# A fifth pair of weight blocks by seven products in the first output product, and new places for the sums made in memory

## The chip, the core and the metric

The kernel runs on one core of a Trainium2 chip. The metric is the device time of one execution, in microseconds; of several executions of one kernel the median is given. All data are 32-bit floats.

## The reference

One layer of an encoder for 256 tokens of 2048 features, cut to the steps that matter:

```python
h = rms_norm(x, attn_norm)
qa, ka, va, qb, kb, vb, ga, gb = split(h @ w_in)
ya = windowed_gqa(qa, ka, va)            # 8 heads of 128
yb = dilated_attention(qb, kb, vb)       # 3 groups of 4 heads, merged to 4 x 128
merged = sigmoid(ga) * (ya @ w_branch_a) + sigmoid(gb) * (yb @ w_branch_b)
x = x + merged @ w_out                   # the output product: 2048 x 2048
hf = rms_norm(x, ffn_norm)
g = dwconv(hf @ w_ffn_gate)
x = x + (gelu(g) * (hf @ w_ffn_up)) @ w_ffn_down
x = x + sigmoid(rms_norm(x, ple_norm) @ w_ple_gate) * (p @ w_ple_proj)
return rms_norm(x, final_norm)
```

The weights dominate: the stream of all their blocks is 258 pieces of 1 MB. The change touches `merged @ w_out`.

## The kernel before

**Precision.** A float32 operand is split in two parts, `hi` (rounded to the matmul's own type) and `lo` (the rest), and a product is made of three matmuls: hi x hi, hi x lo, lo x hi. ScalarE makes `hi` of the weights (L287), VectorE makes `lo` (L288).

**Jobs and pieces.** All matrix products stand in one list of jobs (`_plan`), and their 128x128 weight blocks in one stream (`_stream`), cut in these pieces of 16 blocks. A piece is loaded as two halves of 8 blocks on SP's queue (`load`, L264), into six buffers `raw`; a half is then split into `whi` and `wlo`, of four buffers each (`split_to`). TensorE takes what has been split and releases the buffers. So the whole stream runs as far ahead of TensorE as the buffers let it.

**What is done between.** Everything that is no matmul of the stream is attached to a step of a job: `at((i, k), f)` runs `f` in the program when job `i` comes to its step `k` (`run_due`). The order of the instructions on each engine follows this program order, but a scheduler may move an instruction ahead of or behind others where operands and buffers allow it; instructions in `keep(...)` stay in program order. The jobs that the change speaks of are 34 to 36 (queries), 37, 41, 45 and 47 (`ba`, the branch-A product in four quarters, 8 steps each), 39, 42, 46 and 48 (`bb`, branch B, 4 steps each), 38, 40, 43 and 44 (`gab`, the gates, 16 steps each), and 49 and 50 (`o`, the output product in two halves of its columns, 16 steps each).

**Seven products.** The jobs with eight column blocks (`o`, `gab`, `v8`, `d0`, `d1`, `pgs`) go through `seven_product`. It takes a pair of row blocks of the weights at a time (a piece: 2 row blocks x 8 column blocks) against a pair of feature blocks and the two halves of the tokens. Taken plainly, a pair is eight block products of 128x128 by 128x512, so 24 matmuls. For the pairs in `seven` it uses a scheme with seven block products, so 21 matmuls, in four parts; it needs sums of the weight blocks and sums of the activations. `_pairs` gives the order of the pairs and which go by seven. The partial results are spread over the outputs by `spread_sums`, once, after the last pair by seven of the job (`done`).

- *Sums of weights.* For the jobs before the feed-forward part they are made in memory: `sums_in_memory(j)`, for the j-th pair by seven of the stream, at the step that `MADE_AT[j]` names. It puts a small marker on ScalarE (L330) and POOL (L331), so that the transfers are not issued too soon, and then issues transfers on POOL's queue: a copy of 512 KB (L336), for `w_out` a copy of 256 KB more (L339), two additions in memory of 256 KB (L340, L341) that wait for the copies, and for `w_out` a third (L343) that waits for these. `back` fetches the 512 KB on SP's queue into a buffer `sums` (L356), of which there are three; for `w_out` the other 256 KB go into the second half of the pair's `raw` (L273). The first three fetches of the output product are at step 0 of job 49 (L1152 and L1153), each later one behind part 1 of a pair by seven. The buffers `sums` lie in the pool `ff`, which takes the memory of the attention pool that is closed there (L1146).
- *The four parts.* Part 0 is 4 blocks of `raw`, part 1 the 8 blocks of `sums`, part 2 the first 8 blocks of `raw`, part 3 four blocks that VectorE adds up (L298). TensorE uses them in this order.
- *Sums of activations.* For the output product `add_up` makes them and `early` holds them, as `hi` and `lo`. `merge` calls it: it turns the gated sum `m` by transposes on TensorE (L1022) and splits it into `merged`; from pair 4 (`LATER`) on it also adds up. The merges of quarter 2 are at step 4 of job 47, those of quarter 3 at step 2 of job 49.

Of the kernel before, what the change touches and what calls it, by code (L numbers as in the profile page):

```python
# [10 lines left out]
F32 = mybir.dt.float32  # L11
FR = mybir.dt.float32r
AF = mybir.ActivationFunctionType
ALU = mybir.AluOpType
AX = mybir.AxisListType

P = 128
T = 256
# [19 lines left out]
SUB = 8  # L38
QUARTERS = KC // 4
# [20 lines left out]
def _plan():  # L60
# [48 lines left out]
    for half in range(2):  # L109
# [7 lines left out]
        for c in range(2):  # L117
# [5 lines left out]


TOGETHER = 3
AHEAD = 8 + 5 + 4 * 4
SAVED = 8
SPLIT = 4
ROWS = 7
SHL = 6  # L130
LATER = 4
# [3 lines left out]
FETCHED = ((24, 8), (28, 8), (32, 8), (36, 8), (38, 9), (38, 14), (49, 8), (49, 12))  # L135
MADE_AT = [(9, 1), (10, 8), (11, 14), (13, 4), (14, 12), (16, 14), (18, 2),
           (19, 4), (19, 9), (19, 14), (20, 8), (21, 3), (23, 8), (25, 8), (27, 12), (30, 0), (31, 14),
           (34, 0), (37, 0), (38, 4), (38, 11), (39, 2), (40, 6), (40, 12), (41, 3), (43, 4), (43, 11), (44, 5), (46, 0)]


def _pairs(kind, c):

    if kind == "pgs":
        return [0, 1, 4, 5, 2, 6, 7, 3], range(4, 8)
    if kind == "v8":
        return [0, 1, 2, 4, 3, 5, 6, 7], FARS
    if kind == "gab":
        return [0, 4, 1, 2, 6, 3, 5, 7], GATED
    if kind == "o":
        return ([2, 4, 5, 6, 7, 0, 1, 3] if c else [0, 1, 2, 4, 5, 6, 7, 3]), range(LATER, LATER + 4)  # L150
    if kind == "d1" and c == 1:
        return [5, 0, 1, 6, 2, 3, 7, 4, 8, 9, 10], range(5)
    return [8, 0, 1, 2, 3, 9, 4, 5, 6, 7, 10], range(SAVED)
# [62 lines left out]
def _encoder(ctx: ExitStack, tc, xt, pt, cols, table, onehot, mask, ident_in, last_gain, wts, xrows, out):  # L216
    nc = tc.nc
# [3 lines left out]
    big = ctx.enter_context(tc.tile_pool(name="big", bufs=2))  # L221
# [33 lines left out]
    held = {}  # L255
# [89 lines left out]
    def early_row():  # L345
        return ap_.tile([P, W4], F32, name="row", tag="qf", bufs=4)
# [239 lines left out]
    def at(i, f, *a):  # L586

        due.setdefault(i, []).append((f, a))
# [97 lines left out]
    def view(a, offset, *dims):  # L686
        return bass.AP(tensor=a.tensor, offset=a.offset + offset, ap=[a.ap[0], *([step, n] for step, n in dims)])
# [188 lines left out]
    def add_up(two, out, spare=None):  # L876

        s = (spare_row() if spare is None else spare).rearrange("p (b n) -> p b n", n=P)
        nc.vector.tensor_tensor(view(s, 0, (W4 // 2, 2), (1, P)), view(two, 3 * P, (-3 * P, 2), (1, P)),
                                view(two, P, (0, 2), (1, P)), op=ALU.subtract)  # L880
        nc.vector.scalar_tensor_tensor(s[:, 1], s[:, 0], -1.0, two[:, 0, :P], op0=ALU.mult, op1=ALU.subtract)
        nc.vector.tensor_tensor(s[:, 3], two[:, 1, :P], s[:, 1], op=ALU.add)
        hi, lo = out
        nc.scalar.activation(hi, s, AF.Copy)
        nc.vector.tensor_tensor(lo, s, hi.bitcast(F32), op=ALU.subtract)
# [32 lines left out]
    def spare_row():  # L918
        return row() if "ff" in held else early_row()
# [2 lines left out]
        return [held["shl"][m >= SHL][:, c, :, m % SHL, :] for c in range(2)]  # L922

    def early(m):
        return [held["early"][:, c, :, m - LATER, :] for c in range(2)]

    def row():
        return held["ff"].tile([P, W4], F32, name="row", bufs=ROWS)
# [7 lines left out]
    def spread_sums(kind, n, bank, end, when):  # L936

        by = [rooted(kind, t) for t in range(2)]

        def put(t, c, a):  # L940
            if end and c:
                q = quarter(n, t, c)
                nc.vector.scalar_tensor_tensor(q, a, by[t], q, op0=ALU.mult, op1=ALU.add)
                return
            if kind != "o":
                nc.scalar.activation(a, a, AF.Copy, scale=by[t])
            to_residual(n, t, c, a)

        first, u, v, w = [row() for _ in range(4)]
        nc.scalar.activation(first, bank["p1"], AF.Copy)  # L950
        nc.vector.tensor_tensor(u, bank["p6"], first, op=ALU.add)
        nc.vector.tensor_tensor(v, bank["p7"], u, op=ALU.add)
        for a, b in ((u, u), (w, v)):
            nc.vector.scalar_tensor_tensor(a, bank["p5"], -1.0, b, op0=ALU.mult, op1=ALU.subtract)
        todo = [(0, 0, first), (1, 0, v), (0, 1, u), (1, 1, w)]
        if kind == "o":
            for a in todo:
                put(*a)
            return
        for a, e in zip(todo, when):  # L960
            at(e, put, *a)
# [73 lines left out]

    def rooted(kind, t):
        return 1.0 if kind == "o" else rc[1][:, t:t + 1]

    def joined(n, t, acc, by):

        r = res[:, t, n * W4:(n + 1) * W4]
        nc.vector.scalar_tensor_tensor(r, acc, by, r, op0=ALU.mult, op1=ALU.add)
# [95 lines left out]
    for i, job in enumerate(_JOBS):  # L1138
# [42 lines left out]
        if kind == "gg":  # L1181
            held["asked"] = AHEAD
        if kind == "gg" or (kind == "g" and n == FHALF):
# [2 lines left out]
                j = i + late + (9 * e // 4 if late else 5 * e // 2)  # L1186
                sums_ahead((j, 4), (j + 2, 4))
        if kind == "ba" and n == QUARTERS - 1:
            held["early"] = big.tile([P, 2, 4, QUARTERS, P], FR, name="early", tag="mov", bufs=1)
        if kind == "u" and n % FHALF == FHALF - 2:  # L1190
            for e in range(3):
                at((i, 8), back)
# [52 lines left out]
        elif kind in ("o", "d0", "d1", "gab", "pgs", "v8"):  # L1245
# [3 lines left out]
            if (kind, n) == ("gab", 0):  # L1249
                tags.update(p3="sp", p4="sp", c22="acc", p1="acc", p6="pt", p7="pt", p5="misc")  # L1250
            still, sums_at = {"o": (stills["o"], early), "gab": (stills["v"], of_input), "pgs": (stills["pg"], of_residual),
                               "v8": (stills["v"], of_first)}.get(
                kind, (lambda k: held["act"][:, k, :], shl))
# [23 lines left out]
        elif kind in stills:  # L1277
            tag = {"pg": ("acc", "pt"), "pp": ("sp", "acc"), "ba": ("acc", "sp" if n == 1 else "acc"), "bb": ("pt" if n == 0 else "sp", "pt" if n == 1 else "acc")}[kind][n % 2]
# [18 lines left out]
        elif kind in ("gab", "pgs", "v8"):  # L1297
            th = held["th", "pp" if kind == "pgs" else n]
            for name, a, t in (("p2", "ga", 0), ("p3", "gb", 0), ("p4", "ga", 1), ("c22", "gb", 1)):
# [9 lines left out]
                if n == 0 and a == "ga":  # L1309
                    m = held["m"][:, t, :]  # L1310
# [3 lines left out]
        elif kind in ("o", "d0", "d1"):  # L1314
            parts = held["ss1" if kind == "o" else "ss2"]
            for name, t, c in (("p2", 0, 0), ("p3", 0, 1), ("p4", 1, 0), ("c22", 1, 1)):
                if end:
                    joined(2 * n + c, t, acc[name], rooted(kind, t))
                    squares_of(2 * n + c, t, parts)
                elif kind != "o" and name == "c22":  # L1320
                    joined(2 * n + c, t, acc[name], rooted(kind, t))
                else:
                    a = row()
                    nc.scalar.activation(a, acc[name], AF.Copy, scale=rooted(kind, t))
                    to_residual(n, t, c, a)
            if kind != "d0" and not end:
                at((i + 1, 10), first_squares, parts)
        elif kind == "pg":
            if last:
                last_gates(n, acc, rest)  # L1330
            else:
                for t in range(2):
                    gate(n, t, acc[t], last)
            if n == QUARTERS - 2:
                so_far()
        else:
            after(job, i, acc)
# [51 lines left out]
```

## Time and profile before

| | |
|---|---|
| median of 3 runs | 1443.12 us (1443.11 to 1444.47) |
| the profiled execution, its own time | 1444.3 us |
| its span, first to last instruction | 1442.5 us |
| granted TensorE clock, mean | 0.998 of full speed |
| busy: TensorE, VectorE, ScalarE, POOL | 1431.2, 1183.9, 876.3, 188.3 us |
| moved by DMA | 397.31 MB, 275 GB/s over the span |

The profile is of one execution. Times are in microseconds from the start of the span. A line of the order of time gives the start, the duration, the engine, the source line, the instruction, output and inputs, the number of such instructions, and in brackets the engine's idle time before it with what ended it. "SPq" and "POOLq" are the sequencers that issue transfers. Matmuls are pipelined: the start of one to the start of the next is what one costs, not its duration. A line of the windows gives the stretch, its length, the busy time of TensorE, its weight loads, VectorE, ScalarE and POOL, the granted clock, the busy share of the DMA engines and the GB/s.

### The profile page before, as it was taken

The numbers are of one execution on the slowest core, as the hardware profiler recorded it, in microseconds if no ns is written. First come the engines' busy times: TensorE is split into PE (matmuls) and PEld (weight loads), VectorE is DVE, ScalarE is ACT, GpSimd is POOL, SyncE is SP. The second block draws the span as 40 slices with busy tenths as digits, with TensorE's granted clock in tenths as the row PEclk, the third lists the DMA queues.
The fourth block names the chain that finished last, engine by engine and source line by source line (L and its number), as shares of the span: only waits on it lengthen the run. The fifth ranks groups of instructions, "written<-read, shape, count | busy, mean of one in ns | idle before, by whom it ended". The sixth has DMA issues, their size and how long they took to land.

```text
span 1442.5 us, 21000 instructions
## 1 busy us (share of the span) xinstructions
PE 1431.2 (99%) x7452; PEld 1227.1 (85%) x7452; DVE 1183.9 (82%) x1635; ACT 876.3 (61%) x1256; POOL 188.3 (13%) x291
## 2 busy tenths in 40 slices
PE   9999999999999999999999999999999999999997
PEld 8898888888888888888888888888888888888886
DVE  7798966668879878878888878997888887998896
ACT  7576654456656656775555556776555555677864
POOL 0022222111222110201111100102111110010000
PEclk9999999999999999999999999999999999999999
DMA  9798998889999978968888887989988888799672
GB/s 327 252 244 255 301 292 247 253 231 295 293 295 320 279 238 301 300 220 301 301 287 296 288 300 243 266 292 299 310 307 303 314 302 295 250 294 285 211 240 93
DMA packets 128149, 397.31 MB, mean 275 GB/s; under 512 B 14628, under 2 KB 19876, under 8 KB 127916
## 3 DMA queue, kind: packets, MB, share of 16 engines
q1 hardware_dynamic: 93372, 300.79, 60.4%
q0 software_dynamic: 32656, 91.24, 24.4%
q10 hardware_dynamic: 2016, 3.94, 0.9%
q8 instruction: 58, 0.95, 0.3%
q14 instruction: 47, 0.39, 0.1%
HBM read 363.11 MB, written 58.76 MB: 292 GB/s over the span
## 4 chain that ended last, share of the span: by engine, by line
PE 95%; DVE 2%; DMA 1%; ACT 1%; issue 0%; SPq 0%; POOLq 0%; DVEq 0%; ACTq 0%
PE acc L395 29%; PE acc L398 15%; PE acc L475 12%; PE acc L476 12%; PE acc L474 12%; PE acc L423 3%; PE acc L425 3%; PE acc L424 3%; PE first L372 2%; DMA raw<-in_wts 1%; DVE wlo L288 1%; PE pt L987 1%; PE pt L754 1%; PE acc L447 0%; ACT whi L287 0%
## 5 line engine op out<-in xcount | busy, mean ns | idle before, releaser
L288 DVE TENSOR_TENSOR wlo<-raw,whi 128x1024 fp32r<-128x1024 f32 (+2 forms) x581 | 660.8, 1158 | 94.9 <-ACT whi L287 87.2
L287 ACT ACTIVATE whi<-raw 128x1024 fp32r<-128x1024 f32 (+2 forms) x581 | 573.5, 1005 | 234.6 <-PE acc L476 92.0
L395 PE MATMUL acc<-mov,whi 128*128 128x512 f32 x1840 | 441.3, 391 | 0.0
L395 PEld LDWEIGHTS acc<-mov,whi 128*128 128x128 f32 x1840 | 337.8, 188 | 65.5
L398 PEld LDWEIGHTS acc<-mov,wlo 128*128 128x128 f32 x1840 | 237.3, 191 | 9.0 <-ACT mov L531 0.2
L398 PE MATMUL acc<-mov,wlo 128*128 128x256 f32 x1840 | 243.1, 283 | 0.0
L512 ACT ACTIVATE t<-acc 128x256 f32<-128x256 f32 x115 | 43.6, 379 | 149.6 <-PE acc L395 149.6
L476 PE MATMUL acc<-whi,mov 128*128 128x512 f32 x259 | 100.8, 389 | 0.0
L475 PE MATMUL acc<-wlo,mov 128*128 128x512 f32 x259 | 100.8, 389 | 0.0
L474 PE MATMUL acc<-whi,mov 128*128 128x512 f32 x259 | 100.6, 390 | 0.0
L288 DVE TENSOR_TENSOR wlo<-sums,whi 128x1024 fp32r<-128x1024 f32 x62 | 75.5, 1219 | 8.9 <-ACT whi L287 8.9
L474 PE MATMUL acc<-whi,act 128*128 128x512 f32 x207 | 80.9, 391 | 0.0
L475 PE MATMUL acc<-wlo,act 128*128 128x512 f32 x207 | 80.7, 390 | 0.0
L476 PE MATMUL acc<-whi,act 128*128 128x512 f32 x207 | 80.7, 390 | 0.0
L287 ACT ACTIVATE whi<-sums 128x1024 fp32r<-128x1024 f32 x62 | 65.4, 1056 | 20.4 <-PE acc L476 9.4
L934 POOL DMA_DIRECT2D x<-row x33 | 28.5, 908 | 310.8 <-PE acc L476 106.0
L325 POOL DMA_DIRECT2D kept<-sums x33 | 17.8, 540 | 360.2 <-DVE sums L321 219.4
L475 PE MATMUL acc<-wlo,merged 128*128 128x512 f32 x164 | 64.1, 391 | 0.3 <-DVE wlo L288 0.2
L474 PE MATMUL acc<-whi,merged 128*128 128x512 f32 x164 | 64.0, 390 | 0.0
L476 PE MATMUL acc<-whi,merged 128*128 128x512 f32 x164 | 63.9, 389 | 0.0
L857 ACT ACTIVATE c<-c 128x256 f32<-128x256 f32 x44 | 18.3, 417 | 67.2 <-DVE c L855 67.2
L476 PEld LDWEIGHTS acc<-whi,mov 128*128 128x128 f32 x259 | 48.6, 188 | 10.1
(274 smaller groups left out, 2147.9 us busy)
## 6 DMA issues: line engine op xcount, KB each, us to landing
raw<-in_wts SPq DMA_DIRECT2D x452, 512.0 KB, 6.0
sums<-kept SPq DMA_DIRECT2D x62, 512.0 KB, 5.8
kept<-in_wts POOLq DMA_DIRECT2D x66, 256.0 KB, 8.0
sums<-in_wts POOLq DMA_DIRECT2D x33, 512.0 KB, 7.3
kept<-sums POOLq DMA_DIRECT2D x33, 512.0 KB, 4.6
raw<-in_wts SPq DMA_DIRECT2D x64, 256.0 KB, 5.2
kept<-in_wts POOLq DMA_DIRECT2D x29, 512.0 KB, 7.7
x<-row POOLq DMA_DIRECT2D x33, 256.0 KB, 7.9
```

The lines of the kernel that those rows point to most:

```text
L287: nc.scalar.activation(hi, src, AF.Copy)
L288: ins = nc.vector.tensor_tensor(lo, src, hi.bitcast(F32), op=ALU.subtract)
L372: nc.tensor.matmul(firsts[e][:, T * low:], w, m[:, :2 * T - T * low], start=(k == 0 and not low), stop=(k == KC - 1 and low != turned), sk ...
L395: nc.tensor.matmul(acc, hi[:, k, :], m, start=(first and k == 0), stop=(last and k == SUB - 1), skip_group_check=True)
L398: nc.tensor.matmul(acc[:, T:], lo[:, k, :], m[:, :T], start=False, stop=False, skip_group_check=True)
L423: nc.tensor.matmul(acc, xh, hi, start=(k == 0), stop=False)
L424: nc.tensor.matmul(acc, xh, lo, start=False, stop=False)
L425: nc.tensor.matmul(acc, xl, hi, start=False, stop=(k == n - 1 - t * late))
L474: nc.tensor.matmul(acc, xh, hi, start=(e == 1), stop=False)
L475: nc.tensor.matmul(acc, xh, lo, start=False, stop=False)
L476: nc.tensor.matmul(acc, xl, hi, start=False, stop=(e == uses[name]))
L512: keep(nc.scalar.activation(t, acc[:, T:], AF.Copy, scale=scale))
```

## The change

In half 0 of the output product pair 3 joins the pairs that go by seven products, and pair 2 takes its place as the last pair, by eight. The order becomes 0, 1 by eight, 3, 4, 5, 6, 7 by seven, 2 by eight (before: 0, 1, 2 by eight, 4, 5, 6, 7 by seven, 3 by eight). Half 1 is left as it is. Pair 3 of `merged` was split long before, so its sums of activations are made by a new function, `again`, from `hi` + `lo` of pair 3; it is called at step 4 of job 47. The buffer `early` has one place more.

There is one more set of sums in memory, 30 for 29 (`AHEAD`). The first 17 places in `MADE_AT` stay; the last twelve become thirteen. For the same j: (36, 4) for (37, 0), (37, 4) for (38, 4), (38, 2) for (38, 11), (38, 9) for (39, 2), (39, 2) for (40, 6), (40, 6) for (40, 12), (41, 3) as before, (42, 2) for (43, 4), (43, 6) for (43, 11), (44, 4) for (44, 5), (45, 6) for (46, 0), and (47, 2) new. Since pair 3 comes in between, the sets from (38, 9) on belong to a pair by seven that stands one earlier in the order than the set of the same number before.

```diff
-AHEAD = 8 + 5 + 4 * 4
+AHEAD = 9 + 5 + 4 * 4
...
-           (34, 0), (37, 0), (38, 4), (38, 11), (39, 2), (40, 6), (40, 12), (41, 3), (43, 4), (43, 11), (44, 5), (46, 0)]
+           (34, 0), (36, 4), (37, 4), (38, 2), (38, 9), (39, 2), (40, 6), (41, 3), (42, 2), (43, 6), (44, 4), (45, 6), (47, 2)]
...
-        return ([2, 4, 5, 6, 7, 0, 1, 3] if c else [0, 1, 2, 4, 5, 6, 7, 3]), range(LATER, LATER + 4)
+        return ([2, 4, 5, 6, 7, 0, 1, 3], range(LATER, SUB)) if c else ([0, 1, 3, 4, 5, 6, 7, 2], range(LATER - 1, SUB))
...
-        return [held["early"][:, c, :, m - LATER, :] for c in range(2)]
+        return [held["early"][:, c, :, m - LATER + 1, :] for c in range(2)]
...
+    def again(m):
+        two = spare_row().rearrange("p (c t) -> p c t", t=T)
+        hi, lo = (held["merged"][0][:, 2 * m:2 * m + 2, c:c + T].bitcast(F32) for c in (0, T)) if 2 * m < SPLIT else (
+            held["merged"][1][:, 2 * m - SPLIT:2 * m - SPLIT + 2, c:c + T].bitcast(F32) for c in (0, T))
+        nc.vector.tensor_tensor(two, hi, lo, op=ALU.add)
+        add_up(two, early(m))
...
-            held["early"] = big.tile([P, 2, 4, QUARTERS, P], FR, name="early", tag="mov", bufs=1)
+            held["early"] = big.tile([P, 2, 4, QUARTERS + 1, P], FR, name="early", tag="mov", bufs=1)
+            at((i, 4), again, LATER - 1)
```

## The prediction

> **What bounds the kernel now.** I read the page first, then the idle time of TensorE, then the order of time around the output product.
>
> ```profile
> span 1442.5 us, 21000 instructions
> PE 1431.2 (99%) x7452; PEld 1227.1 (85%) x7452; DVE 1183.9 (82%) x1635; ACT 876.3 (61%) x1256; POOL 188.3 (13%) x291
> ...
> PE 95%; DVE 2%; DMA 1%; ACT 1%; issue 0%; SPq 0%; POOLq 0%; DVEq 0%; ACTq 0%
> ```
>
> TensorE is busy for 99% of the span and carries 95% of the chain of waits. So a matmul less is time won at its full pitch, and any late operand in front of TensorE is time lost. There is almost nothing else to win. Now the order of time on TensorE at the first output product (the job "o", half 0), whose pairs stand in the order 0, 1, 2 by eight and then 4, 5, 6, 7 by seven.
>
> ```profile
> 524.05 1.03 PE L1022 MATMUL pt<-ident,m 128*128 128x128 f32 x8
> ...
> 535.84 0.39 PE L474 MATMUL acc<-whi,merged 128*128 128x512 f32 x1
> ...
> 541.28 1.03 PE L1022 MATMUL pt<-ident,m 128*128 128x128 f32 x8
> ...
> 547.63 0.39 PE L474 MATMUL acc<-whi,merged 128*128 128x512 f32 x1
> ...
> 548.31 0.39 PE L474 MATMUL acc<-whi,merged 128*128 128x512 f32 x1
> 548.54 0.39 PE L475 MATMUL acc<-wlo,merged 128*128 128x512 f32 x1
> ...
> 553.07 0.39 PE L474 MATMUL acc<-whi,merged 128*128 128x512 f32 x1
> ...
> 553.75 0.39 PE L474 MATMUL acc<-whi,early 128*128 128x512 f32 x1
> ```
>
> The 0.39 us is the latency of one matmul; they overlap. A pair by eight is 24 matmuls: from 535.84 to 541.28 that is 5.44 us, 0.2267 us each, and from 547.63 to 553.07 again 5.44. So three pairs take three equal steps, apart from the eight transposes at 541.28. The first pair by seven starts at 553.07 and its first matmul that needs the sums fetched from memory (the second of its four parts, against `early`) starts at 553.75. TensorE waits for nothing here.
>
> **The change part by part.** *Matmuls removed.* Pair 3 goes by seven products: 21 matmuls for 24, so 3 x 0.2267 = **-0.68 us**. It lies wholly on the bound engine. That is 0.05% of the time; a measurement of this kernel can tell about 0.2% (2.9 us) from no change.
>
> *The new sums of activations* (`again`, at step 4 of the last branch-A job, after two merges at the same step). It issues on VectorE one 128x512 add, the three small operations of `add_up` and one 128x512 subtraction, and on ScalarE one 128x512 copy. The merges of before show the same operations:
>
> ```profile
> 527.10 0.42 DVE L879 TENSOR_TENSOR row<-row 128x256 f32<-128x256 f32 x1
> 527.55 0.29 DVE L881 SCALAR_TENSOR_TENSOR row<-row 128x128 f32<-128x128 f32 x1
> ...
> 528.09 0.29 DVE L882 TENSOR_TENSOR row<-row 128x128 f32<-128x128 f32 x1
> ...
> 529.49 1.29 DVE L885 TENSOR_TENSOR early<-row,early 128x512 fp32r<-128x512 f32 x2
> 530.70 1.28 DVE L1011 SCALAR_TENSOR_TENSOR m<-th,acc 128x512 f32<-128x512 f32 x2
> 531.90 2.35 DVE L288 TENSOR_TENSOR wlo<-raw,whi 128x1024 fp32r<-128x1024 f32 x2
> ```
>
> 0.65 for the add (half of the pair of 128x512 operations at 529.49), 0.42 + 0.29 + 0.29, and 0.65: 2.3 us. Queued behind it on VectorE are the two low halves at 531.90. With 2.3 us more the first of them ends at 531.90 + 1.17 + 2.3 = 535.4. They belong to the first two half-pieces of the output product (four buffers of `wlo`, three half-pieces of 2.7 us ahead of TensorE at that time), so TensorE needs the first at 535.84 + 0.23 = 536.07. I take nothing; the cover is about 0.7 us, and if VectorE runs 1 us later than this it costs 0.3. The range of this term is 0 to 0.5.
>
> *The first pair by seven comes one pair sooner.* This is the term that decides. The sums of weights of the first three pairs by seven are fetched by three transfers at the start of this job (`back`, on SP's queue). They go into buffers whose memory belonged to the attention part, and come free only when the last merge's transposes have read it:
>
> ```profile
> 541.36 0.33 SPq L264 DMA_DIRECT2D raw<-in_wts  x1
> 542.35 1.60 SPq L356 DMA_DIRECT2D sums<-kept  x3
> 549.29 0.33 SPq L264 DMA_DIRECT2D raw<-in_wts  x1
> ```
>
> The issue at 542.35 follows the end of the transposes (541.28 + 1.03 = 542.31) at once. These transposes stand at the same step in the changed kernel, so the issue stays where it is. What took the data in:
>
> ```profile
> 549.28 1.06 ACT L287 ACTIVATE whi<-sums 128x1024 fp32r<-128x1024 f32 x1 [1.92 <-DMA sums<-kept]
> ```
>
> ```profile
> 550.37 1.23 DVE L288 TENSOR_TENSOR wlo<-sums,whi 128x1024 fp32r<-128x1024 f32 x1 [0.56 <-ACT whi L287]
> 551.51 0.68 DVE L298 TENSOR_TENSOR raw<-raw 128x512 f32<-128x512 f32 x1
> ```
>
> ScalarE already waits 1.92 us for that first transfer, until 549.28; the low half is done at 551.60, and TensorE needs it at 553.75 + 0.23 = 553.98. Before, 2.4 us of slack hide this. In the changed kernel pair 3 by seven starts at 547.63, and its low half of the sums is needed at **548.54**, 5.44 us sooner. The slack of 2.4 becomes a lack of 3.1 us if the transfer lands as before.
>
> It should land somewhat sooner. The raw load issued at 541.36 (first half of the third pair by seven) stood ahead of the sums. In the changed kernel its buffer comes free only after pair 3's third part, which itself waits for the sums, so it goes behind them. What 512 KB are worth there shows in the transfers between 528 and 560 us, in 40 slices of 0.8 us:
>
> ```profile
> GB/s 205 207 356 251 31 20 0 31 225 277 197 317 238 36 0 179 282 184 179 97 259 341 410 425 415 425 415 282 154 197 282 149 269 292 261 294 187 161 294 213
> ```
>
> From 545.6 to 549.6 it runs at about 415 GB/s, so 512 KB take 1.26 us. The first sums then land at about 549.2 - 1.25 = 547.95. The ends: as before (549.2) where the order does not help, and 546.9 where the load ahead cost twice that. From landing to a finished low half it takes 551.60 - 549.28 + 0.1 = 2.4 us, so the wait is 547.95 + 2.4 - 548.54 = 1.8 us (0.8 to 3.1).
>
> Behind it VectorE is next late: the 128x512 add (0.59 until the next can start) and the low half of the third part (1.17) come after it, 1.75 us, while TensorE has six matmuls, 1.36 us. That adds 0.4. After this VectorE can keep up, but with little to spare:
>
> ```profile
> 535.80:553.10 17.30, 17.30 (x82) 14.37 (x82) 14.26 (x22) 9.22 (x12) 0.00 (x0) 1.00 0.71 250
> 553.10:572.10 19.00, 19.00 (x85) 15.74 (x84) 17.37 (x19) 15.17 (x17) 0.18 (x1) 1.00 0.89 305
> ```
>
> The second row is the four pairs by seven: VectorE (third value) is busy 17.37 of 19.00 us. The fifth such pair in a row costs nothing more by itself; the larger traffic (share of the DMA engines 0.89) fits too. So this step costs 1.8 + 0.4 = **+2.2 us** (1.2 to 3.5).
>
> *The sets of sums in memory.* One more set of five transfers on POOL's queue, and twelve at other steps, all at the same step or sooner for the same number. How long a set takes:
>
> ```profile
> 509.20 1.14 POOL L331 TENSOR_TENSOR edges<-edges,mhalf 128x1 f32<-128x1 f32 x1 [18.15 <-ACT edges L330]
> 510.29 0.56 POOL L336 DMA_DIRECT2D kept<-in_wts  x1
> ...
> 517.00 0.86 POOL L340 DMA_DIRECT2D kept<-in_wts  x1 [5.61 <-DMA kept<-in_wts]
> ...
> 525.09 0.80 POOL L343 DMA_DIRECT2D kept<-kept  x1 [6.36 <-DMA raw<-in_wts]
> ```
>
> The last set of before starts at 509.20 and issues its last addition at 525.09; the additions of that line land in 6.5 us (the line's own times to landing, shortest, median and longest),
>
> ```profile
> DMA to landing us min/median/max: 5.2/6.5/7.8
> ```
>
> so it is done at 532. In the changed kernel this is the last but one, two steps earlier (about 506.5), and the new last one follows on POOL from about 522.4, issues its last addition at 538.3 and is done at 545. Its sums are fetched for the fourth pair by seven of half 1, past 580. So nobody waits for it, and it costs nothing as a wait. Nothing is queued behind it on POOL before the first rows added to the residual, past 570. Behind the ScalarE marker of each set stands only the next split.
>
> As traffic, the moves go into stretches with room (eighth value, the share of the DMA engines):
>
> ```profile
> 300.00:320.00 20.00, 20.00 (x107) 17.13 (x106) 12.53 (x18) 11.39 (x18) 2.40 (x4) 1.00 0.72 198
> 320.00:340.00 20.00, 20.00 (x91) 16.57 (x90) 16.10 (x18) 11.08 (x14) 3.32 (x4) 1.00 0.80 219
> 340.00:360.00 20.00, 19.69 (x86) 15.67 (x85) 17.37 (x22) 12.56 (x15) 2.77 (x4) 1.00 1.02 358
> ...
> 520.00:540.00 20.00, 20.00 (x94) 16.64 (x93) 16.57 (x25) 10.77 (x13) 0.80 (x1) 1.00 0.69 196
> ```
>
> One place can go either way. After the set that starts at 325 us a raw load lands late and TensorE loses about 0.6 us:
>
> ```profile
> 333.45 9.81 DMA raw<-in_wts
> ```
>
> ```profile
> 345.89 0.39 PE L474 MATMUL acc<-whi,merged 128*128 128x512 f32 x1
> 346.51 0.50 PE L475 MATMUL acc<-wlo,merged 128*128 128x512 f32 x1 [0.24 <-DVE wlo L288]
> ```
>
> 345.89 to 346.51 is 0.62 for 0.23. The sets there move up by 7 to 25 us, and one of five transfers takes the place of one of four. I take nothing, with -0.6 to +1.0 as ends.
>
> [...]
>
> **The sum.** -0.68 + 2.2 + 0 + 0 = **+1.5 us**. Against the profiled execution (1444.3 us, 1442.5 of it span) that gives 1445.8; that execution lies 1.2 above the median of the runs, 1443.12, so for the median I say **1444.6**.
>
> **Rivals.** *No wait.* The sums land by 546.1, because the loads ahead were the whole delay (3.8 us from the issue would do). The eight fetches of sums between 530 and 600 us took:
>
> ```profile
> DMA to landing us min/median/max: 4.5/6.7/8.4
> ```
>
> Then only -0.68 is left, or -1.3 if the loss at 345.89 goes too: 1442.4 to 1441.8. For it: the shortest is near 3.8. Against it: none is under it, and the two loads issued just before 541 stay ahead. Chance 0.24.
>
> *Slower, by the late sums.* If the first sums land after 549.3 the wait of 3.2 and the 0.4 behind it outweigh the gain by 2.9. The place is the same; the cause would be the last additions of the new set (538 to 545) on the engines that bring the two raw pairs and the sums, or a later issue on SP. At 550.3: 4.2 + 0.4 - 0.7 = +3.9, so 1447.0. For it: the 9.81 us load beside a set. Against it: the share of 0.69 between 520 and 540. Chance 0.20.
>
> *Faster by more than the matmuls.* The losses beside the moved sets all vanish and none comes in their place: it would take 2.2 us beyond -0.68, and the rows above show TensorE idle for 0.3 us of the 20 from 340 and for none in the others. Chance 0.04: 1440.
>
> **How the numbers follow.** My forecast (+0.3 to +2.8, so 1443.4 to 1445.9) has 0.52, no wait 0.24, slower 0.20, faster 0.04. Within 0.2% are the first two, 0.76. The range reaches from the no-wait case less a little (1441.8) to the middle of the slower one (1446.8).
>
> **What would show it.** Right: at the output product three matmuls less, TensorE and ScalarE both waiting at pair 3's sums, a gap of 1 to 3 us after about 548.3, then one of 0.4, and none in the later pairs by seven. Wrong: no gap there (then I misread what holds the transfer back), a gap at 536 (then `again` is not covered), or raw loads that land late between 310 and 360 or 520 and 545.

## The result and the profile after

The changed kernel takes **1451.1 us** (median of four runs, 1450.41 to 1451.68) beside 1443.3 us for the kernel before on the same chip: a ratio of 1.0048, with a 95% interval of 1.0036 to 1.006. It is 7.8 us slower where +1.5 was forecast. Its profiled execution took 1450.99 us, 1448.9 of it span, so 6.4 us more span than before. (The rest of the 7.8 is 0.3 us more outside the span, 2.1 for 1.8, and that the profiled execution of before lies 1.0 us above its median and this one 0.1 below.) The places below are found in that execution.

The page of the changed kernel: the span and the busy times.

```profile
span 1448.9 us, 21022 instructions
...
PE 1433.7 (99%) x7449; PEld 1227.1 (85%) x7449; DVE 1188.3 (82%) x1643; ACT 878.7 (61%) x1260; POOL 190.5 (13%) x297
```

There are three matmuls fewer (7449 for 7452), and yet TensorE is busy for 2.5 us longer: matmuls that take longer are among the loss, not only waiting. Here is the order of time on TensorE in the changed kernel, from the end of part 0 of pair 3, the first pair by seven.

```profile
549.31 0.39 PE L476 MATMUL acc<-whi,merged 128*128 128x512 f32 x1
552.00 0.73 PE L474 MATMUL acc<-whi,early 128*128 128x512 f32 x2 [2.30 <-ACT whi L287]
553.47 0.50 PE L474 MATMUL acc<-whi,early 128*128 128x512 f32 x1 [0.74 <-ACT whi L287]
...
554.38 0.78 PE L475 MATMUL acc<-wlo,early 128*128 128x512 f32 x1 [0.18 <-DVE wlo L288]
...
555.39 0.63 PE L475 MATMUL acc<-wlo,early 128*128 128x512 f32 x1
555.81 0.63 PE L476 MATMUL acc<-whi,early 128*128 128x512 f32 x1
...
558.16 0.39 PE L474 MATMUL acc<-whi,early 128*128 128x512 f32 x1
```

From 549.31 to 552.00 is 2.69 us for 0.23: a wait for the high half of the fetched sums. Another wait stands before 553.47. Then, behind 554.38, matmuls that wait for nothing follow one another at 0.42 to 0.43 us (555.39 to 555.81) and last 0.63 for 0.39. The windows cut around that stretch name the reason: the last three values are the granted clock, the share of the DMA engines and the GB/s.

```profile
547.60:551.01 3.41, 2.10 (x10) 1.41 (x8) 0.29 (x1) 0.12 (x1) 0.00 (x0) 1.00 1.03 365
551.02:554.42 3.40, 1.50 (x5) 0.64 (x5) 1.92 (x3) 2.40 (x3) 0.00 (x0) 1.00 0.21 84
554.44:557.84 3.40, 3.40 (x8) 2.52 (x9) 3.36 (x4) 2.58 (x3) 0.00 (x0) 0.50 0.61 182
557.85:561.25 3.40, 3.40 (x16) 2.81 (x16) 3.27 (x5) 2.48 (x3) 0.00 (x0) 1.00 0.67 174
```

For 3.4 us TensorE ran at half its clock, and got through 8 matmuls where the next window of the same length has 16. From 549.31 to 558.16 there are 14 steps from matmul to matmul; at 0.2267 they are 3.17 us, and they took 8.85. **Pair 3 lost 5.7 us**: some 1.6 by the clock (in these 3.4 us, a little under half of them) and 4.1 by waits.

Why the sums came late shows on the other engines. The order of time of the changed kernel on POOL (issues of the last two sets), SP (the fetch), ScalarE and VectorE (the split), in this order:

```profile
508.72 0.40 POOL L331 TENSOR_TENSOR edges<-edges,mhalf 128x1 f32<-128x1 f32 x1 [20.74 <-ACT edges L330]
...
526.25 1.26 POOL L331 TENSOR_TENSOR edges<-edges,mhalf 128x1 f32<-128x1 f32 x1
...
543.02 0.81 POOL L343 DMA_DIRECT2D kept<-kept  x1 [6.54 <-DMA kept<-in_wts]
...
543.58 11.14 SPq L356 DMA_DIRECT2D sums<-kept  x4
...
550.89 1.06 ACT L287 ACTIVATE whi<-sums 128x1024 fp32r<-128x1024 f32 x1 [4.33 <-DMA sums<-kept]
551.86 0.61 ACT L884 ACTIVATE early<-row 128x512 fp32r<-128x512 f32 x1
...
552.50 0.69 DVE L885 TENSOR_TENSOR early<-row,early 128x512 fp32r<-128x512 f32 x1 [4.60 <-ACT early L884]
553.11 1.22 DVE L288 TENSOR_TENSOR wlo<-sums,whi 128x1024 fp32r<-128x1024 f32 x1
```

Three things are to be seen. The fetch is issued when the transposes end, as forecast (543.58), but its data is there only at 550.89, 7.3 us later. The last addition in memory of the new set (L343) is issued at 543.02 and so travels beside that fetch. And between the split on ScalarE (done at 551.95) and the low half on VectorE (553.11) stands the last operation of a merge, L885, which itself waits for L884 behind that split on ScalarE. So the low half is done 3.4 us after the landing.

A second new loss lies at the gates, near 491 us. First ScalarE and TensorE in the order of time, then two windows, all of the changed kernel:

```profile
490.21 0.63 ACT L287 ACTIVATE whi<-raw 128x512 fp32r<-128x512 f32 x1 [2.46 <-DMA raw<-in_wts]
...
491.20 0.39 PE L474 MATMUL acc<-whi,mov 128*128 128x512 f32 x1
...
493.36 0.50 PE L475 MATMUL acc<-wlo,merged 128*128 128x512 f32 x1 [0.78 <-DVE wlo L288]
...
495.10 0.50 PE L475 MATMUL acc<-wlo,merged 128*128 128x512 f32 x1
```

```profile
340.00:360.00 20.00, 20.00 (x90) 16.57 (x89) 17.47 (x22) 12.65 (x15) 2.50 (x3) 1.00 1.00 337
480.00:500.00 20.00, 19.12 (x82) 14.84 (x81) 16.14 (x18) 11.62 (x14) 0.81 (x1) 1.00 0.91 238
```

A raw load landed 2.46 us late for ScalarE; ten steps from 491.20 to 495.10 took 3.90 us for 2.27, a loss of 1.6. In exchange the loss at 345.89 of the kernel before is gone (20.00 of 20 us busy, 19.69 before); counted from matmul to matmul over 300 to 350 us that is 0.9.

The sums of activations (`again`), VectorE and then TensorE:

```profile
533.94 1.22 DVE L288 TENSOR_TENSOR wlo<-raw,whi 128x1024 fp32r<-128x1024 f32 x1
...
532.65 0.92 PE L423 MATMUL acc<-whi,yab 128*128 128x512 f32 x2
533.41 0.39 PE L424 MATMUL acc<-wlo,yab 128*128 128x512 f32 x1
```

The low half is done at 535.16, in time for the output product. TensorE loses 0.3 us ahead of it, in branch B: from 532.65 to 533.41 it takes 0.76 us for two steps of 0.23.

By spans: -0.7 (matmuls) - 0.9 (near 346) + 1.6 (near 491) + 0.3 (`again`) + 5.7 (pair 3) = +6.0; the other 0.4 of the 6.4 lies in small pieces of both signs.

### The profile page after: what moved, and what is told of

Its sections match the earlier page's. It is cut to its first block, busy times and chain, and to the rows that moved or that the text cites. A ratio compares the mean times of both kernels' runs of the same rounds, so it can differ in the third digit from the quotient of the medians.

```text
span 1448.9 us, 21022 instructions
## 1 busy us (share of the span) xinstructions
PE 1433.7 (99%) x7449; PEld 1227.1 (85%) x7449; DVE 1188.3 (82%) x1643; ACT 878.7 (61%) x1260; POOL 190.5 (13%) x297
## 4 chain that ended last, share of the span: by engine, by line
PE 59%; DVE 1%; ACT 0%; issue 0%; POOLq 0%; DVEq 0%; ACTq 0%
PE acc L395 22%; PE acc L398 12%; PE acc L475 7%; PE acc L476 7%; PE acc L474 7%; PE acc L425 1%; PE acc L424 1%; PE acc L423 1%; DVE wlo L288 1%; PE pt L987 1%; PE acc L447 0%; DVE raw L298 0%; DVE raw L296 0%; ACT whi L287 0%; DVE row L866 0%
## 5 line engine op out<-in xcount | busy, mean ns | idle before, releaser
L474 PE MATMUL acc<-whi,mov 128*128 128x512 f32 x259 | 100.6, 390 | 0.0
L474 PE MATMUL acc<-whi,act 128*128 128x512 f32 x207 | 80.8, 390 | 0.0
L474 PE MATMUL acc<-whi,merged 128*128 128x512 f32 x159 | 62.4, 392 | 0.0
L476 PE MATMUL acc<-whi,merged 128*128 128x512 f32 x159 | 61.9, 390 | 0.0
L475 PEld LDWEIGHTS acc<-wlo,mov 128*128 128x128 f32 x259 | 48.6, 188 | 10.9 <-DVE wlo L288 0.9
```

The source lines that it names most:

```text
L474: nc.tensor.matmul(acc, xh, hi, start=(e == 1), stop=False)
L475: nc.tensor.matmul(acc, xh, lo, start=False, stop=False)
L476: nc.tensor.matmul(acc, xl, hi, start=False, stop=(e == uses[name]))
```

## The experiments

All differences are of medians against the kernel before on the same chip in the same group of runs; intervals are those of the ratio. Where a kernel has a few lines more, line numbers behind them move by three or so (L477 for L474, L888 for L885).

### One part alone

**again_only**: the kernel before, with `again` and the larger `early`; the new sums are made and not used.

```diff
-            held["early"] = big.tile([P, 2, 4, QUARTERS, P], FR, name="early", tag="mov", bufs=1)
+            held["early"] = big.tile([P, 2, 4, QUARTERS + 1, P], FR, name="early", tag="mov", bufs=1)
+            at((i, 4), again, LATER - 1)
```

> The kernel before, which also makes the sums of activations of pair 3 at step 4 of job 47 and does not use them. Theory A: 0 to +0.3 us (covered; at most the 0.2 us seen near 533 us in the changed kernel). Theory C (the added work on VectorE and ScalarE pushes the splits of the output product back): +2 us or more, with waits between 535 and 556 us.

Measured: +0.4 us, 1.0005 (0.9996 to 1.0015). Its profile has the same 0.3 us, at 532.53, and no other loss beside those of the kernel before. `again` is not the cause.

**places_only**: the kernel before with its last twelve sets at the new places (ten of them move), without the thirteenth.

```diff
-           (34, 0), (37, 0), (38, 4), (38, 11), (39, 2), (40, 6), (40, 12), (41, 3), (43, 4), (43, 11), (44, 5), (46, 0)]
+           (34, 0), (36, 4), (37, 4), (38, 2), (38, 9), (39, 2), (40, 6), (41, 3), (42, 2), (43, 6), (44, 4), (45, 6)]
```

> The kernel before with the first twelve of the new places for its last twelve sets; nothing else. Theory A: the loss of 0.9 us near 346 us goes, one of 1.5 to 1.8 us near 491 us comes, nothing at the output product: +0.5 to +1 us. Theory B: most of the 6 to 8 us is here, +4 us or more.

Measured: -0.7 us, 0.9997 (0.9988 to 1.0007). In its windows no idle time is left near 346 and none has come near 491; a smaller loss (0.65 us) came at 366:

```profile
340.00:360.00 20.00, 20.00 (x90) 16.57 (x89) 16.28 (x19) 11.67 (x13) 2.52 (x3) 1.00 1.00 323
480.00:500.00 20.00, 20.00 (x90) 16.57 (x89) 18.01 (x19) 12.87 (x15) 1.52 (x2) 1.00 0.89 262
```

So the new places by themselves do no measurable harm; the loss that was expected near 491 is not in this execution.

**order_only**: the kernel before, with the four pairs by seven one place sooner and pair 2 behind them. No fifth pair, no `again`, no new set.

```diff
-        return ([2, 4, 5, 6, 7, 0, 1, 3] if c else [0, 1, 2, 4, 5, 6, 7, 3]), range(LATER, LATER + 4)
+        return ([2, 4, 5, 6, 7, 0, 1, 3] if c else [0, 1, 4, 5, 6, 7, 2, 3]), range(LATER, LATER + 4)
```

> Computes the same as the kernel before; only the order of the pairs in half 0 differs (0, 1, then 4 to 7 by seven, then 2 and 3 by eight), so the first pair by seven comes one pair sooner; no matmul is saved, no set is added or moved. Theory A (the sums of the first pair by seven land too late, and TensorE's clock falls to half behind the wait): +2 to +6 us, with a wait of 1.5 to 2.5 us at the first matmul with the sums, and a granted clock near 0.5 for 3.4 us behind it if that wait is long enough. Theory B (the loss comes from the traffic of the moved and added sets): 0 to +1 us, no clock below 1.

Measured: +2.8 us, 1.002 (1.001 to 1.0029). The order of time on SP, ScalarE, VectorE and TensorE:

```profile
540.92 8.53 SPq L356 DMA_DIRECT2D sums<-kept  x4
...
545.62 1.06 ACT L287 ACTIVATE whi<-sums 128x1024 fp32r<-128x1024 f32 x1 [1.71 <-DMA sums<-kept]
...
547.23 0.69 DVE L885 TENSOR_TENSOR early<-row,early 128x512 fp32r<-128x512 f32 x1 [1.99 <-ACT early L884]
547.84 1.22 DVE L288 TENSOR_TENSOR wlo<-sums,whi 128x1024 fp32r<-128x1024 f32 x1
...
550.86 0.50 PE L474 MATMUL acc<-whi,merged 128*128 128x512 f32 x1 [0.55 <-ACT whi L287]
```

The late sums alone make a loss: three waits of 0.85, 0.35 and 0.71 us in this profile, shorter than the expected 1.5 to 2.5, and 2.3 us in all with the longer steps behind each (nine steps from 546.89 to 551.20 took 4.31 us for 2.04), at the full clock. The sums land 4.7 us after the issue, with no addition in memory beside them, and yet L885 again holds back the low half (549.06, 3.4 us after the landing). This profiled execution (1445.59 us) is one of the shortest of its ten; what the others lose beyond it was not profiled.

### The late sums taken away

**early_fetch**: the changed kernel, with the first two sums fetched a job earlier (step 0 of job 48) into room behind `early`, so that they need not wait for the transposes.

```diff
-            held["early"] = big.tile([P, 2, 4, QUARTERS + 1, P], FR, name="early", tag="mov", bufs=1)
+            room = big.tile([P, 5 * SUB + 3 * SUB, P], FR, name="early", tag="mov", bufs=1)
...
+            held["room"] = [room[:, (5 + e) * SUB:(6 + e) * SUB, :].bitcast(F32) for e in range(2)]
+            for e in range(2):
+                at((i + 1, 0), back)
...
-            for e in range(3):
+            for e in range(1):
```

> The changed kernel, with the sums of the first two pairs by seven fetched into spare room of the tile that holds the sums of activations, at step 0 of job 48 instead of step 0 of job 49; the others as they were. Theory A: no wait at pair 3, the clock stays at 1.00, and of the 6.4 us of span between the changed kernel and the one before 5 to 6 are won back: +0.3 to +1.5 us against the kernel before (the loss near 491 us stays). Theory B: still +5 us or more.

Measured: +1.35 us, 1.0012 (1.0002 to 1.0021). That takes most of the 7.8 us away. No stretch at half clock is left at pair 3: behind its waits the matmuls follow one another at 0.23 us (549.30 to 550.00). What is left there is 0.3 us, behind the low half that still stands behind L885's operation, and 0.5 us, behind a high half of a raw load: ScalarE had waited 2.55 us for a transfer before it.

**defer**: the changed kernel; the last two merges make their sums of activations at steps 5 and 8 of job 49, so L884 and L885 no longer stand between the high and the low half of the first sums.

```diff
-        add_up(two, early(2 * n + e))
+        at((_O, (5, 8)[e]), add_up, two, early(2 * n + e)) if late else add_up(two, early(2 * n + e))
```

> The changed kernel with the adding up of pairs 6 and 7 (the second half of the last two merges) at steps 5 and 8 of job 49 for step 2, so that on VectorE the last operation of a merge no longer stands ahead of the low half of pair 3's sums, and on ScalarE its copy no longer between two splits of pair 3. Theory F (that order costs 1.1 us behind the landing): the low half ends about 2.4 us behind the landing of the sums, for 3.5: +5 to +7 us, and +3 to +5 if the shorter wait leaves the clock at 1.00. If the order does not matter: as the changed kernel.

Measured: +4.9 us, 1.0034 (1.0021 to 1.0047); the changed kernel in the same group (**after_again**, below) +6.3. ScalarE and VectorE:

```profile
550.67 1.06 ACT L287 ACTIVATE whi<-sums 128x1024 fp32r<-128x1024 f32 x1 [3.67 <-DMA sums<-kept]
...
551.76 1.23 DVE L288 TENSOR_TENSOR wlo<-sums,whi 128x1024 fp32r<-128x1024 f32 x1 [3.15 <-ACT whi L287]
```

The low half is now done 2.3 us after the landing instead of 3.4: the order in the queues is worth 1.1 us. The half clock stays (553.3 to 556.7), and the pair's 13 steps from 550.03 to 557.26 lose 4.3 us for 5.7.

**early_defer**, both together, with the new places:

> The early fetch of the first two sums and the later adding up together. If the late landing, the order on VectorE and ScalarE, and the halved clock are all there is at the output product, no gap is left there and the 0.7 us of the saved matmuls show: -0.7 to +1.0 us against the kernel before (the loss near 491 us may stay). If a gap of over 0.5 us is left at the output product, something else is late there.

Measured: +2.0 us, 1.0015 (1.0006 to 1.0024), where at most +1.0 was expected. In the profiled execution (1444.68 us, 1.1 below the median of its ten) nothing is lost at pair 3, neither by waits nor by the clock. What is left is near 491, as this window shows; what the longer executions lose beyond it was not profiled:

```profile
480.00:500.00 20.00, 19.14 (x83) 15.02 (x82) 16.36 (x19) 11.41 (x13) 0.81 (x1) 1.00 0.85 240
```

**after_again**, the changed kernel once more:

> The changed kernel once more, beside the others of this group. Expected: +6 to +8 us against the kernel before; two gaps on TensorE at pair 3's sums, of about 2.5 and 0.9 us, and the granted clock at a half for about 3.4 us behind them, if these belong to the kernel and not to one execution. The loss near 491 us (1.7 us in the first profile) is expected to vary.

Measured: +6.3 us, 1.0042 (1.0028 to 1.0057). Its profiled execution (1452.77 us) has a wait of 2.57 us at the same place and the half clock for twice as long, 6.8 us; and it loses 2.4 us near 366, where the first one has no loss.

### The new set beside the fetch

**set_sooner**: the changed kernel with its last two sets at (45, 0) and (45, 6) for (45, 6) and (47, 2).

> The changed kernel with its last two sets at (45, 0) and (45, 6) for (45, 6) and (47, 2), so that the last addition in memory is issued near 531 us for 543 us, clear of the fetch of the first sums. Theory D (that addition, which runs beside the fetch, makes the sums 1.5 us later): the sums land under 6 us from their issue (7.3 in the changed kernel), the first gap is near 1 us for 2.5, the clock stays at 1.00: +2 to +4 us. Theory E (the fetch is late by its issue alone, and the added set does not matter): +6 to +8 us.

Measured: +4.8 us, 1.0031 (1.0018 to 1.0044). Inconclusive: the markers slid behind the same gates on ScalarE, POOL's last addition was still issued at 543.33, and the sums landed 6.6 us after their issue.

**set_clear**: the last three sets at (44, 4), (44, 11) and (45, 6).

```diff
-           ... (43, 6), (44, 4), (45, 6), (47, 2)]
+           ... (43, 6), (44, 4), (44, 11), (45, 6)]
```

> The changed kernel with its last two sets at (44, 11) and (45, 6) for (45, 6) and (47, 2): in set_sooner the markers slid behind the same gates on ScalarE and POOL's last addition stayed at 543 us, so that edit did not test the point. Here only one set is left behind 508 us and its last addition is issued near 525. Theory D (the added set's last addition, beside the fetch, makes the first sums late): they land 4.5 to 5.5 us from their issue, as with the order alone (4.7), the first gap is under 1 us, the clock stays at 1.00, and the output product loses 1.5 to 2.5 us for 6: +2 to +4 us (with more loss near 491 us, as a set is moved there). Theory E (the set does not matter): 6.5 us or more to landing, the clock at a half, +6 us or more.

Measured: +5.4 us, 1.0042 (1.0027 to 1.0057). POOL, SP, ScalarE:

```profile
527.01 0.81 POOL L343 DMA_DIRECT2D kept<-kept  x1 [6.44 <-DMA raw<-in_wts]
...
544.06 1.29 SPq L356 DMA_DIRECT2D sums<-kept  x3
...
549.69 1.06 ACT L287 ACTIVATE whi<-sums 128x1024 fp32r<-128x1024 f32 x1 [2.64 <-DMA sums<-kept]
```

With the last addition done long before, the fetch takes 5.6 us for 7.3: 1.7 us, and the first wait shrinks from 2.5 to 0.8. Pair 3's 14 steps from 549.79 to 557.05 still lose 4.1 us: the half clock came all the same (3.4 us of it), against the expectation, and the low half still stands behind L885. Another 1.6 us are lost near 366. These are readings of one execution of each kernel; by the median (+5.4 for +6.3, on different chips) it can't be told from the changed kernel.

### The places, once the late sums are gone

**after_old_places**: the changed kernel, the twelve old places and (47, 2).

> The changed kernel with the old twelve places and (47, 2) as the thirteenth: pair 3, the new sums and one more set, but nothing moved. If the moved places cost about 1 us (the loss near 491) and the rest is at the output product: +5 to +7 us, no loss near 491, the loss of 0.6 us near 346 back, the half clock still there. If the moves cost nothing: as the changed kernel, +6 to +8.

Measured: +4.1 us, 1.0032 (1.0021 to 1.0044). The loss near 491 is gone and 0.25 us near 347 is left; at pair 3 there are waits of 1.28, 0.91 and 0.35 us and 3.4 us of half clock. The fetch took 6.1 us, again beside an addition (issued at 542.83).

**early_defer_old**: early_defer with the old places and (47, 2).

> The early fetch and the later adding up, with the old twelve places and (47, 2). No gap at the output product, no loss near 491: -1 to +0.5 us against the kernel before, so that the 0.7 us of the saved matmuls show in the trace at least. If it stays at +2 us as with the new places, the places are not the cause of what early_defer lost.

Measured: 0.0 us, 1.0002 (0.9992 to 1.0011). TensorE is busy without a break where the changed kernel lost 5.7 us:

```profile
535.80:553.10 17.30, 17.30 (x82) 14.41 (x81) 15.10 (x24) 10.44 (x14) 2.50 (x3) 1.00 0.93 293
```

A loss of 0.8 us near 346 is left.

To see which of the moved sets makes the loss near 491, two kernels mix the places of early_defer: **first_new** has the new ones up to (41, 3) and the old ones behind, **last_new** the other way round.

> This is early_defer (the changed kernel with the first two sums fetched early into spare room and the last two merges' last operations put later) with the sets of sums in memory that go through the stream up to job 41 at their new places and the later ones at their old places. If the late places make the loss near 491 us (0.94 + 0.25 us in early_defer) and the early ones only take away the loss at 346 us (0.58 + 0.24 us in early_defer_old): neither loss is there, and the time is -1.2 to +0.3 us against the kernel before. Rival, the early places make it: the loss near 491 us stays and the time is +1 to +2.5 us.

> early_defer with the sets up to job 41 at their old places and the later ones at their new places. If the late places make the loss near 491 us: a loss of 0.9 to 1.7 us there and one of 0.6 to 0.9 us near 346 us, time +1 to +2.5 us against the kernel before. Rival, the early places make it: no loss near 491 us, time -0.5 to +0.7 us.

Measured: first_new -0.35 us, 1.0001 (0.9991 to 1.0011); last_new +1.2 us, 1.0009 (1.0 to 1.0019). In the profiled executions, 1443.33 and 1443.26 us, neither has a loss near 346 or 491. Their windows from 300 to 400 and from 480 to 500 us, first_new and then last_new:

```profile
300.00:400.00 100.00, 100.00 (x464) 83.25 (x464) 81.57 (x97) 60.46 (x77) 19.18 (x28) 1.00 0.93 291
480.00:500.00 20.00, 20.00 (x90) 16.56 (x89) 18.00 (x20) 12.75 (x15) 2.52 (x3) 1.00 0.96 274
```

```profile
300.00:400.00 100.00, 100.00 (x464) 83.34 (x463) 82.39 (x98) 60.46 (x78) 18.32 (x27) 1.00 0.89 277
480.00:500.00 20.00, 20.00 (x90) 16.57 (x89) 18.00 (x20) 12.83 (x15) 1.19 (x2) 1.00 0.93 257
```

The expected 0.9 to 1.7 us of last_new near 491 was not there. But its ten runs go from 1443.26 to 1446.42, those of first_new from 1442.57 to 1447.53: such losses come in some executions and not in others, and a profile is one execution. Medians lean to the late places as the cause (+1.2 for -0.35, with intervals that overlap); it stays open.

All sixteen profiles (the kernel before, the changed one twice, the other runs), one execution each, say a little more, counted from matmul to matmul:

- Near 491 the seven with new places throughout (as changed, or with the last ones sooner, as in set_sooner and set_clear) and a thirteenth set lose 0.3 to 2.2 us. The nine others lose nothing, places_only, first_new and last_new among them.
- Near 346 four of the seven with the old places up to (41, 3) lose 0.7 to 1.3 us, and three lose 0.1 or nothing, order_only and last_new among these. None of the nine with the new ones loses anything there, but three of these lose 0.8 to 2.4 us near 366.

None of these kernels is measurably faster than the one before.

### The clock by itself

**gaps**: the kernel before with twelve reductions on VectorE in the feed-forward part, of 128 x 512n with n from 5 to 16, their results unused. They hold back the low halves, so TensorE waits for some microseconds at places that have nothing to do with the change. One run.

```diff
+    def lag(n):
+        keep(nc.vector.tensor_reduce(row()[:, :1], held["hf"][:, :n, :].rearrange("p k t -> p (k t)").bitcast(F32), axis=AX.X, op=ALU.max))
...
+        if i in GAPS:
+            at((i, 4), lag, GAPS[i])
```

> The kernel before with twelve single VectorE reductions over 128 x 512n elements in the feed-forward part (n from 5 to 16, so about 2.7 to 8.5 us each, 33 us apart), whose results are not used; they hold back the low halves of the weights, so TensorE waits for them, from not at all to some 4 us. Theory G (a long enough wait of TensorE sets its clock to a half for 3.4 us): behind the long waits, and not behind the short ones, the granted clock is a half for multiples of 3.4 us; the first wait with it tells how long is enough, between 1.3 and 3 us by the runs so far. If no wait here does it, the half clock behind pair 3's sums has another cause.

Measured: 1474.71 us. TensorE in the order of time, and four windows:

```profile
749.73 1.22 PE L399 MATMUL acc<-mov,wlo 128*128 128x256 f32 x8 [1.66 <-DVE wlo L289]
...
847.75 0.58 PE L399 MATMUL acc<-mov,wlo 128*128 128x256 f32 x1 [4.39 <-DVE wlo L289]
...
1177.26 2.90 PE L396 MATMUL acc<-mov,whi 128*128 128x512 f32 x6 [5.68 <-DVE u L517]
```

```profile
746.34:749.74 3.40, 1.75 (x13) 1.43 (x11) 3.40 (x7) 2.62 (x5) 1.52 (x3) 1.00 0.48 190
841.92:845.31 3.39, 1.44 (x7) 0.85 (x5) 3.39 (x1) 0.00 (x0) 0.00 (x0) 1.00 0.41 156
845.33:848.73 3.40, 0.97 (x4) 0.98 (x5) 3.40 (x6) 0.63 (x1) 0.00 (x0) 0.50 0.04 6
848.74:852.14 3.40, 3.40 (x12) 2.88 (x11) 3.40 (x4) 1.55 (x2) 0.00 (x0) 0.50 0.74 225
```

A wait of 1.66 us leaves the clock alone (1.00 from 747 to 757 us); in waits of 4.39 and 5.68 us it drops before the wait ends (at 845.3 and 1176.4), to half for some 6.8 us each. So the half clock does not need the changed code; here it came in waits of TensorE.

## Why the prediction was wrong

Its mechanism was right: pair 3 waits for sums that come late, both on ScalarE and on TensorE, at the place that was named. What failed is the size of the step *The first pair by seven comes one pair sooner*, put at +2.2 us (1.2 to 3.5) and measured at **5.7**; with 1.6 us near 491 beside it, the time left the range.

- **Matmuls removed**, -0.68: right, 7449 for 7452.
- **`again`**, 0 (0 to 0.5): right: 0.3 us, alone and in the changed kernel, though in branch B and not at 536, where the cover was worked out.
- **The landing**: put at 547.95 in the time of the kernel before (546.9 to 549.2). The changed kernel runs 1.23 us behind there (transposes at 542.51 for 541.28), so 550.89 is 549.66: 1.7 us too late, and out of the range. The prediction took the raw load away that had stood ahead of the fetch, and got 5.6 us from issue to landing. Without an addition beside the fetch set_clear shows just that, 5.6, and order_only 4.7. But in the changed kernel an addition in memory came beside it: 7.3 us here, 7.4 in after_again, 6.6 in set_sooner, 6.4 in defer, 6.1 in after_old_places. (The early end of the term, a load ahead that cost twice 1.25 us, is 546.7 and not 546.9; this changes nothing here.)
- **Why it came beside it** is the failed sentence of *The sets of sums in memory*: the last set but one was to start two steps earlier, at 506.5, and the new one to be done at 545. On POOL the last but one started at 508.72, where the kernel before has 509.20: POOL waited 20.74 us for its marker on ScalarE, so a place two steps sooner did not make it sooner. The new set stood behind it on POOL's queue until 526.25 (522.4 had been worked out), and its last addition went out at 543.02, not 538.3. "Nobody waits for it" was true, and "it costs nothing" was not: the addition ran beside the fetch, which took 7.3 us here and 5.6 in set_clear, where no addition ran beside it.
- **From the landing to the low half**: 2.4 us were read in the kernel before, where the last merge was done before the sums landed (L885 ended at 548.08, the sums were there at 549.28). One pair sooner the split of the sums stands ahead of the merge's L884 on ScalarE, and L885, which waits for L884, ahead of the low half on VectorE. It took 3.4 us in the changed kernel and in order_only, and 2.3 in defer: 1.1 us that no row of the prediction had.
- **The wait** of 1.8 + 0.4 so became some 4.1: the low half was 2.8 us later than predicted, of which TensorE took some by matmuls of the high half ahead of their turn. In order_only, without the new set, the same step lost 2.3 us in the profile, near the 2.2.
- **The clock** was missing from the sum: 1.6 us here. It came behind waits of 2.30, 0.74 and 0.18 us, while order_only, with 0.68, 0.18 and 0.55, kept the full clock; so the step was not linear in the lateness. early_fetch, which takes the long wait away, takes it away too.
- **The moved sets**, 0 (-0.6 to +1.0): the gain near 346 came (-0.9), and a raw load landed late near 491 instead (+1.6), where the prediction had not looked: net +0.7, within the ends, but from two losses of which it knew one. places_only gives -0.7 for the places alone; which set makes the loss near 491, and why some executions are without it, is open.

The rival that was realized is *Slower, by the late sums* (0.20): its condition (landing past 549.3) and its cause (the last additions of the new set) were named. At 549.66 it would have given 3.5 + 0.4 - 0.7 = +3.2; the queues, the clock and the loss near 491 are what was short. Its counter-argument, a share of 0.69 for the DMA engines from 520 to 540, was read in the kernel before, without the new set, and ahead of the fetch. *No wait* (-0.7) is what early_defer_old comes near once the wait is taken away: 0.0, which this measurement can't tell from -0.7.

## What to carry to other kernels

When a step is made earlier, list what else stands in each of its queues at the new time, operations that were already done at the old time included, and what is in flight on the DMA engines at the moment of its fetch; a place in a program is not a time, and a marker behind a gate stays where the gate is. Price waits in front of a dense TensorE stream with the clock in mind: three short ones close together (0.61, 0.74 and 0.18 us in set_clear) had 3.4 us of half clock behind them, and with one of 2.41 us in after_again came 6.8 us. And take a gain of 0.7 us only where the operands are there with more slack than the scatter of a transfer, here 4.7 to 7.4 us for the same 512 KB.

## What the runs showed of the hardware

TensorE's clock was halved with waits, short ones too, for 3.41 us in the changed kernel (554.43 to 557.84) and for some 6.8 us in after_again and, three times, in gaps (from 845.3, 1060.4 and 1176.4). At half clock the matmuls of 128x512 followed one another at 0.43 us for 0.23 in the changed kernel. Here are waits with a drop behind them or in them, and some without, as the brackets of the order of time give them (by the steps from matmul to matmul those of order_only are some 0.17 us longer), and the time at half clock:

| kernel | waits of TensorE, us | at half clock, us |
|---|---|---|
| changed kernel | 2.30, 0.74, 0.18 | 3.41 |
| after_again | 2.41 | 6.8 |
| defer | 1.36, 0.76 | 3.4 |
| after_old_places | 1.12, 0.74, 0.18 | 3.4 |
| set_clear | 0.61, 0.74, 0.18 | 3.4 |
| order_only | 0.68, 0.18, 0.55 | none |
| gaps, at 749.73 | 1.66 | none |
| gaps, at 847.75 | 4.39 | 6.8 |
| gaps, at 1177.26 | 5.68 | 6.8 |

One more row without a drop, from order_only, with waits in it; the first value behind the comma is TensorE's busy time.

```profile
547.00:550.41 3.41, 2.45 (x9) 1.05 (x7) 3.18 (x4) 1.81 (x3) 0.00 (x0) 1.00 0.18 42
```

And two of set_clear, the one that ended in a drop and the one behind it:

```profile
550.01:553.41 3.40, 1.87 (x6) 0.83 (x6) 2.11 (x3) 2.20 (x3) 0.00 (x0) 1.00 0.33 135
553.43:556.83 3.40, 3.40 (x9) 2.25 (x9) 3.36 (x5) 2.52 (x3) 0.00 (x0) 0.50 0.63 180
```

It is not the longest wait that divides these cases: 0.74 us was the longest in set_clear, while gaps got by with a single one of 1.66. Nor is it their sum: 1.53 us in set_clear, with a drop, and 1.41 in order_only and 1.66 in gaps, without. Nor TensorE's busy time in 3.4 us: of the rows shown 1.75 us (gaps, mostly matmuls of 128x256) stands without a drop, and 1.87 (set_clear) with one. It is not the same in every execution either: the changed kernel's first wait was 2.30 us in one profile and 2.41 in the other, and the half clock lasted 3.41 and 6.8 us. What decides whether the clock drops, and for how long, is not shown by these runs; nor is it shown whether this makes the runs of order_only scatter.
